# A hybrid decoder layer on one core: plain products in the first third of the tokens, weight sums formed over two thirds, quads accumulating in one bank

## The chip, the cores and the metric

The kernel runs on one core of one Trainium2 chip. The metric is device time in microseconds: the median of the timed runs. A core has a tensor engine (PE) that multiplies into PSUM (eight banks of 128 partitions x 512 fp32), a vector engine (DVE), a scalar engine (ACT), GpSimd (POOL), which does not take part in reading PSUM here, and SyncE (SP), whose queue issues every transfer of this kernel in the order of the program.

## The reference

One layer for 2048 prompt tokens and 8 x 8 sample tokens (2112 in all), width 1024, everything in fp32:

```python
xn = rms_norm(x, norm_pre)
z = einsum('btd,de->bte', xn, w_in)            # 1024 -> 4096
v_pool, g_pool, u_lru, g_lru = four blocks of 1024 columns of z
y_pool = causal multi-scale pooling of v_pool (windows 2, 4, 8, 16), a map per group, a scale
y_lru  = width-4 causal convolution of u_lru, then a gated linear recurrence (scan over tokens)
mixed  = concat(y_pool * silu(g_pool), y_lru * silu(g_lru))      # 2048
out    = einsum('bte,ed->btd', mixed, w_out)   # 2048 -> 1024
return x + rms_norm(out, norm_post), and the new states
```

## The kernel before

**Precision.** An fp32 operand is split into a high part (a copy to fp32r, usually on ACT) and a low part (a subtraction, on DVE or POOL); `split` (lines 127 to 132) does both. A product is high x high, high x low and low x high, three matmuls. `quad_product` (342) does this over four blocks of 128 rows: twelve matmuls of 128x128 by 128x352.

**Stages.** The tokens are cut in three thirds of 704 (m = 0, 1, 2). A start stage loads and normalizes the first third and makes the first pair of blocks of each of V, G and U by plain products (`z_pair`). Then come the quads of the three thirds in the order of `QUADS` (704 to 715), then an output stage (from 1582) that multiplies the stored `mixed` by `w_out`. This output stage works on sums of blocks of `w_out`, which `combos_chain` (1245) forms ahead and stores in `wtd`.

**A quad** is (m, p, kind): two blocks of 128 output columns (j = 0, 1) of one kind (V the pool input, G its gate, U the recurrent input, L its gate) over the 704 tokens (two halves of 352, c = 0, 1), with the inner 1024 in two halves (h = 0, 1). As a 2x2 matrix product it is made with seven products instead of eight (Winograd's form of Strassen's scheme), at the price of sums: of x (named T1 to T4, beside the plain quarters X11, X21, X22) and of the weights. `ORDER` gives the order of the products, `XOF` the x operand of each. `quad_slot` (863) issues one product and returns its evacuation: PSUM banks a, b, e, c, d, the intermediate sums in a tile `q` (`t["tmp"]`), five additions on DVE (516 ns each) and two copies on ACT. Product 2 accumulates onto bank a (used by product 1) and product 3 onto bank e (used by product 5); these carry line 236, the others 238.

**Weights.** For each quad of the first third, and the first three of the second, `w_step` (742) forms the four sums on DVE and splits the seven operands: the high parts on ACT, four low parts on POOL (`LO_POOL`) and three on DVE. Where m < 2 the split operands (512 KB each) are stored to `wsd`; all later quads load them from there. A weight step is taken seven products ahead of its use (`AHEAD`), in eight buffers (`W_BUFS`).

**Order of the work.** The program is written out by hand inside `manual_schedule`: each engine runs its queue in that order. `one_slot` (1284) is one product's time: it issues the product, then the evacuations of the slot before, one waiting map or gate from `pe_q`, due stores (`later`), and then as much of the side chains (`gens`, sorted by rank) as the planned budget of 1.92 us per engine allows (`run_gens`). The side chains are `pool_chain`, `silu_chain`, `conv_chain`, `lru_chain`, `x_chain` (normalizes the next third), `combos_chain` and `region_chain`. Weight steps and the `transition` (1202), which forms the next third's x operands during the last quad of a third and the first of the next, stand ahead of the slot's evacuations. Before a quad the program puts in empty slots until enough tiles are free (line 1499).

The main loop, in short:

```python
for n in range(7 * len(QUADS)):
    qi, i = divmod(n, 7)
    ...
    ws = w_step(n + AHEAD)
    one_slot(body, [a + b for a, b in zip(tr, ws)])
```

Of the kernel before, what the change touches and what calls it, by code (L numbers as in the profile page):

```python
# [18 lines left out]
KT = D // P  # L19
# [40 lines left out]
SLOTS = ("A", "B", "X11", "T2", "T1", "T3", "T4", "X21", "X22")  # L60
# [4 lines left out]
def hymba_kernel(  # L65
# [650 lines left out]
    LATE_PREP = [(1, 0, kind) for kind in "VGU"]  # L716
    PREP = [q for q in QUADS if q[0] == 0] + LATE_PREP
# [13 lines left out]
    def w_raw(q, names):  # L731
        if q is None:
            return
        _, p, kind = q
        for n in names:
            blk, h = blocks(kind, p)[int(n[0]) - 1], int(n[1]) - 1
            t = (raw_tile if n[0] == "1" else tp_tile)(f"wr{kind}{p}_{n}")
            w_rawt[q, n] = w_load_raw(blk, h, t)

    LO_POOL = (0, 3, 5, 6)  # L740

    def w_step(n):
        if n >= 7 * len(QUADS):
            return 0.0, 0.0, 0.0
        q, i = QUADS[n // 7], n % 7
        m, p, kind = q
        key = (KINDS[kind] // 8 * NG + p) * 7 + i
        t = w_tiles[n] = half_tile(f"w{m}{kind}{p}_{i}")
        flat = t.rearrange("p a b -> p (a b)").bitcast(F32)
        if q not in PREP:  # L750
            nc.sync.dma_start(out=flat, in_=wsd[:, key, :])
            return 0.0, 0.0, 0.0
        nxt = PREP[PREP.index(q) + 1] if q != PREP[-1] else None
        r = {n_: w_rawt.get((q, n_)) for n_ in ("11", "12", "21", "22", "s1", "s2", "s4")}
        cost = 0.65
        if i == 0:
            src = r["11"]
        elif i == 1:
            s1 = w_rawt[q, "s1"] = raw_tile(f"s1{kind}{p}")
            src = w_rawt[q, "s2"] = tp_tile(f"s2{kind}{p}")  # L760
            tadd(s1, r["21"], r["22"])
            tsub(src, s1, r["11"])
            cost += 1.3
        elif i == 2:
            src = r["s1"]
            tsub(r["21"], r["11"], r["21"])
            cost += 0.65
            w_raw(nxt, ("11",))
        elif i == 3:
            src = r["21"]  # L770
        elif i == 4:
            src = r["22"]
            s4 = w_rawt[q, "s4"] = raw_tile(f"s4{kind}{p}")
            tsub(s4, r["12"], r["s2"])
            cost += 0.65
        elif i == 5:
            src = r["12"]
        else:
            src = r["s4"]
        pool = i in LO_POOL  # L780
        split(t[:, 0, :], t[:, 1, :], src, AC, G if pool else V)
        if i == 3:
            w_raw(nxt, ("21",))
        elif i == 4:
            w_raw(nxt, ("22",))
        elif i == 5:
            w_raw(nxt, ("12",))
        if m < LM:
            later(2, lambda: nc.sync.dma_start(out=wsd[:, key, :], in_=flat))
        return cost - (0.65 if pool else 0.0), 0.62, (1.35 if pool else 0.0)  # L790
# [65 lines left out]
    def put_sum(q, j, c, a, b, op=ALU.add):  # L856
        for out, lo, hi, is8 in dst_parts(q, j, c):
            i0, i1 = a[:, lo:hi], b[:, lo:hi]
            if is8:
                i0, i1 = as8(i0), as8(i1)  # L860
            V.tensor_tensor(out=out, in0=i0, in1=i1, op=op)

    def quad_slot(q, i, n):
        t = Q[q]
        pid = ORDER[i]
        w = w_tiles.pop(n)
        name = XOF[pid]
        c0 = CW

        def bank(key):  # L870
            t[key] = z_psum(f"{key}{n}")[:, :CW]
            return t[key]

        def U(i):
            return t["tmp"][:, i * CW:(i + 1) * CW]

        if pid == 1:
# [10 lines left out]
        elif pid == 5:  # L888
            quad_product(bank("e"), w, name, True, True)

            def evac():
                pass
# [819 lines left out]
```

## Time and profile before

| | |
|---|---|
| runs | 1345.55, 1342.72, 1345.72 us; median 1345.55 |
| profiled execution | 1339.65 us, of which 1337.9 are the span from first to last instruction |
| busy, share of the span | PE 86%, weight load 80%, DVE 74%, ACT 48%, POOL 35% |
| transfers | 324.73 MB, 243 GB/s on average |
| granted clock of PE | 0.926 on average |

How to read the views: the list of lines groups instructions by line, engine and tile, with count, total time, mean nanoseconds of one, and the idle time of the engine just before them with who ended it. The list of waits has total, times and longest in microseconds. A row of the timeline has start, length, engine, line, and in brackets how long the engine stood idle before it. A weight tile is named by third and kind: `w0L` is a tile of kind L in the first third. Matmul ends in the timeline are modelled and overlap the next start; the distance of two starts is the time of one group.

### The profile page before, as it was taken

The numbers are of one execution on the slowest core, as the hardware profiler recorded it, in microseconds if no ns is written. First come the engines' busy times: TensorE is split into PE (matmuls) and PEld (weight loads), VectorE is DVE, ScalarE is ACT, GpSimd is POOL, SyncE is SP. The second block draws the span as 40 slices with busy tenths as digits, with TensorE's granted clock in tenths as the row PEclk, the third lists the DMA queues.
The fourth block names the chain that finished last, engine by engine and source line by source line (L and its number), as shares of the span: only waits on it lengthen the run. The fifth ranks groups of instructions, "written<-read, shape, count | busy, mean of one in ns | idle before, by whom it ended". The sixth has DMA issues, their size and how long they took to land. (4 is left out here: it accounts for less than half of the span.)

```text
span 1337.9 us, 17719 instructions
## 1 busy us (share of the span) xinstructions
PE 1152.4 (86%) x6118; PEld 1069.0 (80%) x6118; DVE 990.3 (74%) x1370; ACT 645.8 (48%) x1031; POOL 463.9 (35%) x408
## 2 busy tenths in 40 slices
PE   7949678857757699989899979899987999999996
PEld 6949678747757699989889869899975888887775
DVE  7899688888788568767676854857556758677668
ACT  5353757625643775444546452727654333334322
POOL 3366464554456323232244322424310002221222
PEclk9979779868878899989899979999988999999998
DMA  8067586945665799979789777978658966657653
GB/s 308 26 222 286 184 318 241 359 181 187 228 226 202 272 330 354 354 242 383 235 315 333 265 262 250 325 254 278 206 170 236 269 183 187 182 165 233 183 166 110
DMA packets 172010, 324.73 MB, mean 243 GB/s; under 512 B 17360, under 2 KB 79056, under 8 KB 171920
## 3 DMA queue, kind: packets, MB, share of 16 engines
q1 hardware_dynamic: 171920, 323.59, 70.8%
q8 instruction: 48, 0.79, 0.2%
q14 instruction: 42, 0.34, 0.1%
HBM read 221.13 MB, written 102.15 MB: 242 GB/s over the span
## 5 line engine op out<-in xcount | busy, mean ns | idle before, releaser
L442 PE MATMUL p<-XN,s 128*128 128x512 f32 (+1 forms) x224 | 88.3, 394 | 8.9 <-ACT s L129 8.7
L1059 DVE SCALAR_TENSOR_TENSOR xs<-u,parT,xs 128x704 f32<-128x704 f32 (+1 forms) x72 | 88.3, 1227 | 3.8 <-ACT xs L1049 2.6
L444 PE MATMUL p<-XN,s 128*128 128x512 f32 (+1 forms) x224 | 88.0, 393 | 2.0 <-DVE s L132 2.0
L443 PE MATMUL p<-XN,s 128*128 128x512 f32 (+1 forms) x224 | 88.2, 394 | 0.4 <-DVE XN L132 0.2
L1100 POOL TENSOR_TENSOR ig<-ig,xs 128x704 f32<-128x704 f32 (+1 forms) x24 | 46.2, 1927 | 94.7 <-ACT ig L1099 80.6
L435 POOL TENSOR_TENSOR xr<-acw,xr 128x512 f32<-128x512 f32 x8 | 13.1, 1641 | 185.9 <-DVE acw L575 123.5
L238 PE MATMUL y<-dh,pw 128*128 128x352 f32 x192 | 56.5, 339 | 15.5 <-ACT pw L129 14.9
L307 POOL TENSOR_TENSOR xl<-xs,xh 128x704 fp32r<-128x704 f32 (+1 forms) x24 | 45.6, 1902 | 66.6 <-ACT xh L1064 53.4
L435 POOL TENSOR_TENSOR xr<-ac,xr 128x512 f32<-128x512 f32 x19 | 35.6, 1887 | 79.8 <-issue 52.2
L435 DVE TENSOR_TENSOR a<-a,a 128x512 f32<-128x512 f32 x48 | 34.0, 714 | 37.0 <-DMA a<-mixed 32.4
L129 ACT CAST s<-a 128x512 fp32r<-128x512 f32 x48 | 28.6, 618 | 67.1 <-DVE a L435 48.9
L1064 ACT CAST xh<-xs 128x704 fp32r<-128x704 f32 (+1 forms) x24 | 18.9, 788 | 86.1 <-DVE xs L1059 86.1
L238 PE MATMUL z<-XN,w 128*128 128x352 f32 x288 | 53.3, 347 | 7.4 <-ACT w L1316 5.4
L442 PEld LDWEIGHTS p<-XN,s 128*128 128x128 f32 x224 | 43.0, 192 | 19.3 <-ACT s L129 9.1
L238 PEld LDWEIGHTS z<-XN,w 128*128 128x128 f32 x288 | 49.9, 203 | 10.3 <-ACT w L1316 5.4
L1108 DVE SCALAR_TENSOR_TENSOR w<-rg,xs 128x704 f32<-128x704 f32 (+1 forms) x24 | 22.9, 955 | 43.5 <-ACT xs L1105 36.8
L444 PE MATMUL p<-XN,a 128*128 128x512 f32 x137 | 54.3, 396 | 0.1
L442 PE MATMUL p<-XN,a 128*128 128x512 f32 x137 | 54.2, 396 | 0.0
L443 PE MATMUL p<-XN,a 128*128 128x512 f32 x137 | 54.2, 395 | 0.0
L444 PEld LDWEIGHTS p<-XN,s 128*128 128x128 f32 x224 | 42.9, 191 | 12.2 <-DVE s L132 2.7
L310 DVE TENSOR_TENSOR q<-b,q 128x352 f32<-128x352 f32 x45 | 23.2, 517 | 38.8 <-PE b L238 37.2
L443 PEld LDWEIGHTS p<-XN,s 128*128 128x128 f32 x224 | 43.0, 192 | 10.7 <-DVE XN L132 1.1
(481 smaller groups left out, 3704.0 us busy)
## 6 DMA issues: line engine op xcount, KB each, us to landing
a<-mixed SPq DMA_DIRECT2D x112, 256.0 KB, 4.2
mixed<-g SPq DMA_DIRECT2D x48, 352.0 KB, 5.0
wsd<-w0L SPq DMA_DIRECT2D x28, 512.0 KB, 4.9
w1L<-wsd SPq DMA_DIRECT2D x28, 512.0 KB, 6.0
w2V<-wsd SPq DMA_DIRECT2D x28, 512.0 KB, 5.7
w2G<-wsd SPq DMA_DIRECT2D x28, 512.0 KB, 5.8
w2U<-wsd SPq DMA_DIRECT2D x28, 512.0 KB, 4.9
w2L<-wsd SPq DMA_DIRECT2D x28, 512.0 KB, 7.1
```

Source lines behind the costliest of these rows:

```text
L129: hi_eng.copy(out=hi, in_=src)
L238: nc.tensor.matmul(out, lhsT=lhsT, rhs=rhs, start=start, stop=stop)
L307: (eng or V).tensor_tensor(out=out, in0=a, in1=b, op=ALU.subtract)
L310: (eng or V).tensor_tensor(out=out, in0=a, in1=b, op=ALU.add)
L435: (eng or nc.vector).tensor_tensor(out=out, in0=a, in1=b, op=op)
L442: nc.tensor.matmul(out, lhsT=ah, rhs=wh, start=start and k == 0, stop=False)
L443: nc.tensor.matmul(out, lhsT=ah, rhs=wl, start=False, stop=False)
L444: nc.tensor.matmul(out, lhsT=al, rhs=wh, start=False, stop=stop and k == KT - 1)
L1059: V.scalar_tensor_tensor(out=xs, in0=E[:, k:k + n], scalar=col(C_CW + 8 * k, b), in1=xs, op0=ALU.mult, op1=ALU.add)
L1064: AC.copy(out=xh, in_=xs)
L1100: G.tensor_tensor(out=gi, in0=gi, in1=v, op=ALU.mult)
L1108: V.scalar_tensor_tensor(out=u, in0=r, scalar=1.0, in1=v, op0=ALU.add, op1=ALU.mult)
```

## The change

- In the first third a quad is made of its eight plain products. Two products (h = 0, 1) accumulate in one bank, and four copies on ACT take the banks out. No sums of x and no sums of weights are needed for it: each quad splits four weight tiles, one quad ahead (`plain_tile`, in slots 4 to 7), three of which are stored for later thirds.
- The weight sums for the later thirds are formed in the first third for the six V and G quads (`s_prep`, in slots 0 to 3, into x regions that lie idle) and in the second third for its ten other quads (`is_late`), which load their three plain operands from `wsd` and form and store four others.
- All low parts of weights are formed on DVE; none on POOL.
- In the later thirds, products 1, 6, 7 and 4 accumulate in one bank a, and 5 and 3 in e; after each, the running result is copied by ACT or added into its place by DVE. A quad has four copies on ACT and three additions on DVE, and needs no tile `q`.
- The x operands of a third are formed in another order, and those of the start stage are the four plain quarters; the start stage stores its split weights too.
- The sums of `w_out` (`combos_chain`) move from the second third to the last, load one step ahead and wait less; `region_chain` starts earlier there.

The diff, cut to its core:

```diff
-AHEAD = 7
-ORDER = (1, 6, 5, 7, 4, 2, 3)
+ORDER = (1, 5, 6, 3, 7, 2, 4)
...
+    EARLY = "VG"
+    def is_late(q):
+        return q[0] == 1 and (q[1] == 0 or q[2] not in EARLY)
...
+    PLAIN_PID = {"11": 1, "12": 2, "22": 4}
+    IDLE = [XN[:, BASE[n] + 1024 * i:BASE[n] + 1024 * (i + 1)] for n in ("X11", "T2", "T1") for i in range(2)]
...
+    def plain_tile(q, n):
+        t = w_tiles[q, n] = half_tile(f"w{q[2]}{q[1]}_{n}")
+        split(t[:, 0, :], t[:, 1, :], w_rawt[q, n], AC, V)
+        if n in PLAIN_PID:
+            store_w(flat_of(t), q[2], q[1], PLAIN_PID[n])
+        return 0.65, 0.62, 0.0
...
+    def s_sums(q, i):
+        r11, r12, r21, r22 = (w_rawt[q, n] for n in NAMES)
+        if i == 0:
+            tadd(r22, r21, r22)
+        elif i == 1:
+            tsub(r21, r11, r21)
+        elif i == 2:
+            tsub(r11, r22, r11)
+        else:
+            tsub(r12, r12, r11)
...
+    def s_prep(q, i):
+        if q[2] not in EARLY:
             return 0.0, 0.0, 0.0
+        s_sums(q, i)
+        dve, act = 0.65, 0.0
+        for pid in ((), (5,), (6, 7), (3,))[i]:
+            b = IDLE[n_idle[0] % len(IDLE)]
+            n_idle[0] += 1
+            split(b[:, :512], b[:, 512:], w_rawt[q, S_OF[pid]], AC, V)
+            store_w(b, q[2], q[1], pid)
+            dve, act = dve + 0.65, act + 0.62
+        return dve, act, 0.0
+
+    def w_step(q, i):
         m, p, kind = q
+        pid = ORDER[i]
+        t = w_tiles[q, pid] = half_tile(f"w{m}{kind}{p}_{pid}")
+        if not is_late(q) or pid in (1, 2, 4):
+            key = (KINDS[kind] // 8 * NG + p) * 7 + pid - 1
+            nc.sync.dma_start(out=flat_of(t).bitcast(F32), in_=wsd[:, key, :])
+        if not is_late(q) or i > 4:
             return 0.0, 0.0, 0.0
+        if i < 4:
+            s_sums(q, i)
+        if not i:
+            return 0.65, 0.0, 0.0
+        split(t[:, 0, :], t[:, 1, :], w_rawt[q, S_OF[pid]], AC, V)
+        store_w(flat_of(t), kind, p, pid)
+        return 1.3 if i < 4 else 0.65, 0.62, 0.0
...
+    PLAIN = [(j, h, c) for c in range(2) for j in range(2) for h in range(2)]
+    PLAIN_X = {(0, 0): "X22", (1, 0): "T3", (0, 1): "X21", (1, 1): "T4"}
+    def plain_slot(q, i):
...
+        if h == 0:
+            t["z"] = z_psum(f"z{q[2]}{q[1]}_{i}")[:, :CW]
+        quad_product(t["z"], w, PLAIN_X[h, c], h == 0, h == 1)
...
+            if h:
+                put_copy(q, j, c, z)
...
+        key = {1: "a", 6: "a", 7: "a", 4: "a", 5: "e", 3: "e", 2: "d"}[pid]
+        first = pid in (1, 5, 2)
+        if first:
+            t[key] = z_psum(f"{key}{q[0]}{q[2]}{q[1]}")[:, :CW]
+        z = t[key]
+        quad_product(z, w, XOF[pid], first, True, True)
+
+        def evac():
+            if pid == 1:
+                put_copy(q, 0, 0, z)
+            elif pid == 5:
+                put_copy(q, 1, 1, z)
+            elif pid == 6:
+                put_copy(q, 0, 1, z)
+            elif pid == 3:
+                put_sum(q, 0, 1, z)
+            elif pid == 7:
+                put_sum(q, 1, 1, z)
+            elif pid == 2:
+                put_sum(q, 0, 0, z)
+            else:
+                put_copy(q, 1, 0, z)
+                quad_end(q)
...
+        plan = {0: (("X11",), ("T1",), ("t1", "T2"), ("t2",), ("X22-", "T3"), ("t3",), ("T4",), ("X21-",), ("4", "t4")),
...
     def combos_chain():
-        for k in range(KT):
+        def load(k):
...
+        nxt = load(0)
+        yield 0, 0, 0, 3
+        for k in range(KT):
+            r, nxt = nxt, load(k + 1) if k + 1 < KT else None
...
+                yield 0.65, 0, 0, 0
+            yield 0, 0, 0, 3
...
+        def start_store(kind, b):
+            for n, pid in PLAIN_PID.items():
+                store_w(flat_of(wt[b + int(n[0]) - 1, int(n[1]) - 1]), kind, 0, pid, 0)
+            due_dmas()
...
+        def prep(n, qi, i):
+            if QUADS[qi][0] == 0:
+                if i < 4:
+                    return s_prep(QUADS[qi], i)
+                if qi < lasts[0]:
+                    return plain_tile(QUADS[qi + 1], NAMES[i - 4])
+                if i == 4:
+                    for s in steps[:3]:
+                        w_step(*s)
+                return w_step(*steps[i - 1])
+            n = n - i0 + 7
+            return w_step(*steps[n]) if n < len(steps) else (0.0, 0.0, 0.0)
...
-                while t_free() < {"V": 1}.get(q[2], 3) or (q[2] == "V" and (e_free() < 2 or not sums_done(*q[:2]))):
+                while t_free() < {"V": 0}.get(q[2], 2) or (q[2] == "V" and (e_free() < 2 or not sums_done(*q[:2]))):
...
+                if qi + 1 < len(QUADS) and QUADS[qi + 1][0] == 0:
+                    w_raw(QUADS[qi + 1])
+                if qi + 2 < len(QUADS) and is_late(QUADS[qi + 2]):
+                    w_raw(QUADS[qi + 2])
...
-            if m == 1 and (qi, i) == (lasts[0] + 5, 0):
-                spawn(combos_chain(), 0, rank=3)
             if m == 2 and (qi, i) == (lasts[1] + 2, 0):
+                spawn(region_chain(0, "b11", 0, 5), 0, rank=2)
+                spawn(combos_chain(), 20, rank=2)
```

More of the change, by code (lines that the diff above doesn't have):

```diff
@@ new lines, in store_w, with flat_of @@
+    def store_w(flat, kind, p, pid, slots=2):
+        key = (KINDS[kind] // 8 * NG + p) * 7 + pid - 1
+        later(slots, lambda: nc.sync.dma_start(out=wsd[:, key, :], in_=flat.bitcast(F32)))
+    def flat_of(t):
+        return t.rearrange("p a b -> p (a b)")
+    def plain_tile(q, n):
[4 more added lines that the diff above has]
+        return 0.65, 0.62, 0.0
@@ L1263, in region_chain @@
+                later(2, lambda j=j, k=k, o=r[o]: nc.sync.dma_start(out=wtd[:, j, k, :], in_=o))
+                yield 0.65, 0, 0, 0
+            yield 0, 0, 0, 3
     def region_chain(r, j, k0, k1):
@@ L1444, in hymba_kernel @@
         scaled("G", ZG0, 0)
+        start_store("V", 0)
         for b in (16, 17):
```

256 lines of the change are left out of this document (79 added, 177 removed).

## Prediction

> **What bounds the kernel now.** I read the page's busy shares and slices first, then split the span into stages where the matmul timeline shows the first product of each third.
>
> ```profile
> PE 1152.4 (86%) x6118; PEld 1069.0 (80%) x6118; DVE 990.3 (74%) x1370; ACT 645.8 (48%) x1031; POOL 463.9 (35%) x408
> PE   7949678857757699989899979899987999999996
> PEclk9979779868878899989899979999988999999998
> ```
>
> ```profile
> 0.00:63.51 63.51, 55.11 (x302) 51.96 (x303) 48.26 (x98) 28.08 (x63) 24.24 (x40) 1.00 0.49 171
> 63.51:391.05 327.54, 232.22 (x1253) 225.15 (x1251) 276.14 (x307) 178.46 (x274) 174.96 (x122) 0.84 0.67 244
> 391.05:691.74 300.69, 267.51 (x1576) 264.40 (x1576) 218.25 (x259) 155.58 (x222) 99.50 (x88) 0.94 0.83 299
> 691.74:969.20 277.46, 258.18 (x1549) 255.53 (x1548) 187.49 (x252) 146.42 (x199) 102.46 (x122) 0.96 0.78 268
> 969.20:1337.90 368.70, 339.39 (x1444) 271.98 (x1444) 260.18 (x458) 137.22 (x275) 62.72 (x39) 0.96 0.64 189
> ```
>
> The columns are length; PE, weight load, DVE, ACT, POOL busy; clock; DMA share; GB/s. The page's PE share of 86% is an average over unlike stages: the first third's 13 quads take longer (327.54) than the second's 16 (300.69) or the last's 16 (277.46), at the lowest clock, with DVE at 276.14/327.54 = 0.84 and POOL at its highest. What a quad must cost PE shows in undisturbed products:
>
> ```profile
> 105.37 2.08 PE L238 MATMUL b<-XN,w0V 128*128 128x352 f32 x12
> 107.29 2.08 PE L238 MATMUL e<-XN,w0V 128*128 128x352 f32 x12
> ...
> 487.79 0.32 PE L238 MATMUL r<-xh,lw 128*128 128x352 f32 x1
> 488.75 2.08 PE L238 MATMUL b<-XN,w1G 128*128 128x352 f32 x12
> ```
>
> Starts are 1.92 us apart, so seven products are 13.44; a map or gate between two products (487.79 to 488.75) is 0.96. A third has 16 map and 16 gate groups; from the loops, the first third's window holds about 24 of its 32, the rest falls into the next. PE's own work is thus 13 x 13.44 + 24 x 0.96 = 197.8 in the first third and 16 x 13.44 + 32 x 0.96 = 245.8 in the others. Lost: 129.8, 54.9 and 31.7 us. Who was waited for in the first third, by the list of waits (total, times, longest):
>
> ```profile
> PE e L236 <- DVE g L861: 42.4, 7, 11.6
> PE e L236 <- DVE e L861: 10.1, 3, 4.9
> PE a L236 <- ACT q L882: 8.9, 2, 7.6
> ```
>
> and in the second and the last:
>
> ```profile
> PE e L236 <- DVE g L861: 19.2, 5, 7.9
> ...
> PE e L236 <- DVE g L861: 9.5, 2, 5.5
> ```
>
> The seventh product accumulates in bank e, which must first be read by DVE; DVE is late. Each long wait is paid twice:
>
> ```profile
> 98.77 3.89 PE L236 MATMUL e<-XN,w0L 128*128 128x352 f32 x12 [4.45 <-DVE g L861]
> ...
> 119.36 2.19 PE L236 MATMUL e<-XN,w0V 128*128 128x352 f32 x12 [1.32 <-DVE e L861]
> ```
>
> After 4.45 us idle a product takes 3.89 instead of 2.08; after 1.32 it takes 2.19. The Trainium skill (TensorE: Matmul & The Clock Gate, "What's actually happening") says the clock halves after an idle window of about 3.4 us and returns after as long a busy one; the trace agrees. Why DVE is late:
>
> ```profile
> L310 DVE TENSOR_TENSOR s1G<-wrG,wrG 128x512 f32<-128x512 f32 x3 | 5.6, 1868 | 0.0
> L310 DVE TENSOR_TENSOR s1L<-wrL,wrL 128x512 f32<-128x512 f32 x3 | 2.0, 678 | 0.0
> ...
> L310 DVE TENSOR_TENSOR q<-b,q 128x352 f32<-128x352 f32 x13 | 6.7, 515 | 0.0
> ```
>
> On ACT and on POOL in the same third:
>
> ```profile
> L129 ACT CAST w0L<-wrL 128x512 fp32r<-128x512 f32 x15 | 8.8, 610 | 1.2 <-DVE wrL L307 1.2
> L882 ACT COPY q<-a 128x352 f32<-128x352 f32 x13 | 5.8, 445 | 0.0
> ```
>
> ```profile
> L132 POOL TENSOR_TENSOR w0L<-wrL,w0L 128x512 fp32r<-128x512 f32 x11 | 22.6, 2057 | 39.6 <-ACT w0L L129 39.3 <-POOL u L838 0.3
> L132 POOL TENSOR_TENSOR w0G<-wrG,w0G 128x512 fp32r<-128x512 f32 x9 | 13.4, 1496 | 4.4 <-ACT w0G L129 3.1 <-DMA swd<-lw 1.3
> ```
>
> The same sum takes 678 ns in one place and 1868 in another, and this third is where POOL is busy for 174.96 us. The Trainium skill (SBUF — State Buffer, "Who interferes with whom") calls it an exclusive port: a DVE instruction with two inputs in SBUF and a POOL instruction reading SBUF exclude each other. The two rows fit that.
>
> **First third, part by part.** PE: eight products instead of seven, 13 x 1.92 = +25.0; own work 222.7. The 13 x 5 additions on PSUM leave DVE (65 x 0.515 = -33.5); four copies per quad take their place on ACT, two more than now (26 x 0.445 = +11.6 there, beside PE work). Weights on DVE: 98 instructions now (13 x 7, and 7 of the next third's first quad), after it 13 x 4 low parts, 6 x 8 for sums and splits of the V and G quads, 8 ahead: 108. Their price lies between 0.678 and 1.868; now they come to some 96 us (29 rows, of which s1G and s1L above are the dearest and one of the cheapest), 0.98 each. I take 0.85, since some 54 POOL splits between 1.5 and 2.06 us, some 94 of its 175 us, go: 92 us. At 0.68 it would be 73, at 0.98 106. The first quad no longer needs sums of x (about a dozen instructions of 0.8 to 1.6 us, -10). DVE's other 136 us should lose a tenth to the quieter port (bounds nothing and a fifth): -14. DVE: 276.1 - 33.5 - 4 - 10 - 14 = 215. By the rule of the Trainium skill's SBUF page alone, the instructions freed from POOL would all run at their lone price: an estimate of some 180 us, with PE the only bound.
>
> The wait that carried the loss is gone: two products share a bank, no product accumulates on a bank that has been read, and a weight tile is split four slots (7.7 us) before it is used, which replaces "seven ahead". At today's 0.84 DVE share 215 us make 255 us; PE's 222.7 plus the 31.7 that the last third loses make 254. I take 255, -72.5; ends 231 (8 us lost) and 289 (242.6 us of DVE, nothing gained in its prices, at 0.84). The 39 us that the first quad takes now (63.51 to 102.45) fall to near 16 in this: its x parts are plain halves, the last two are needed only from the fifth product on.
>
> **SP's queue and the stores.** Nine 512 KB stores of the start's weights go into SP's queue ahead of the raw loads of the first quad; a wait there for a split holds those loads back. PE has the two last products of the start to run meanwhile (48 matmuls of 0.16 us each, 15.4 us together), so I cost it at nothing; without that cover a few us. In the third itself stores fall from 91 to 63.
>
> **Second third.** Ten quads instead of three form sums here. Without the 8 instructions done ahead (7 now) these are 72 on DVE instead of 14: at 0.85 each 61 us against some 15. Off DVE: 16 x 2 additions (-16.5), and the output weights' sums, 20 of which lie here:
>
> ```profile
> L307 DVE TENSOR_TENSOR wo<-wo,wo 128x512 f32<-128x512 f32 x20 | 22.3, 1115 | 0.1
> ```
>
> and by the list of DMA issues:
>
> ```profile
> wo<-in_w_out SPq DMA_DIRECT2D x32, 256.0 KB, 6.0
> wtd<-wo SPq DMA_DIRECT2D x32, 256.0 KB, 5.8
> ```
>
> DVE: 218.3 + 46 - 16.5 - 22.3 = 225. ACT: 16 x 2 copies (+14) and 22 splits (+13): 183. The new wait is the shared bank: products 1, 6, 7, 4 run in bank a, each after the evacuation of the one before, with one product (1.92 us) between; 3 follows 5 likewise. Today product 2 comes four products after product 1 in bank a, and product 3 has two products between it and the one (7) whose evacuation reads bank e. Behind a waiting product stands all of PE's queue, maps and gates too, and the sums on DVE wait for those. The evacuations are queued on ACT and DVE behind weight splits, where ACT itself waits for DVE's sums. How late they come today:
>
> ```profile
> 426.48 2.10 PE L238 MATMUL a<-XN,w1G 128*128 128x352 f32 x12
> 436.69 0.45 ACT L882 COPY q<-a 128x352 f32<-128x352 f32 x1
> ...
> 535.60 2.09 PE L238 MATMUL a<-XN,w1V 128*128 128x352 f32 x12
> 537.73 0.45 ACT L882 COPY q<-a 128x352 f32<-128x352 f32 x1 [5.34 <-PE a L238]
> ```
>
> The product that ends at 428.58 is copied by 437.14, 8.6 us later; the other by 0.5. I took this lag for product 1 (ACT) and 7 (DVE) in all 32 quads of both later thirds; these two pairs are among the longest and shortest. What exceeds 1.92 us, the larger of both per quad, sums to 44.5 and 33.2; by the present two-product allowance it is 30.7 and 23.7. So the tighter chain costs about +14 and +10. Against that, the second third starts without the backlog of the first, and its x sums are formed in the order of use while plain products still run: I take -15. DVE's extra 7 us fall beside PE work. 300 us; ends 277 (the last third's loss) and 322 (nothing won at its start, chain and DVE's 7 on the path).
>
> **Last third.** +10 for the chain, -16.5 on DVE for additions, +20 sums of the output weights at 0.68 to 1.12 (14 to 22 us): DVE level. All 64 transfers of 256 KB now fall here, at up to twice their pace (a set of four sums needs about five slots instead of nine). The 40 of them that lie earlier today are 10.5 MB; with the present 268 GB/s x 277.46 us = 74.4 MB that makes 298 GB/s over 285 us, less than:
>
> ```profile
> 468.56:567.40 98.84, 98.38 (x616) 97.90 (x615) 74.42 (x99) 54.93 (x83) 28.95 (x29) 1.00 0.95 346
> ```
>
> where PE did not wait. But in their stretch of some 80 us, 2.1 MB per five slots on top of 268 is beyond 346. Weights are asked for seven products (13.4 us) ahead, so I charge little: 288; ends 270 (chain at nothing, additions saved) and 310 (the chain's 10 and 22 of sums on the path). Start and output stage keep 63.5 and 368.7.
>
> **Sum.** 63.5 + 255 + 300 + 288 + 368.7 = 1275 span, +1.75 around it: 1277, against the profiled 1339.65. The median shown, 1345.55, lies 0.4% above that execution; I stay near the profiled frame and say 1276.
>
> **Rivals.** *PE-bound throughout*: if DVE runs free of POOL as the 678 ns row has it, the first third takes 240, the second 277, the last 270: 63.5 + 240 + 277 + 270 + 368.7 + 1.75 = 1221. For: DVE's room; against: 0.84 without slack. 12%. *DVE stays the pace of the first third*: with prices unchanged 289, total 1311. For: six quads have twelve DVE instructions each. 10%. *Transfers of the output weights collide with weight loads in the last third*: 310 there, 1299. 8%.
>
> *The shared bank locks PE to ACT and DVE* (the slower end): the ten quads with sums then run at the first third's present pace, 327.54/13 = 25.2 us, instead of 300.69/16 = 18.8: +64; the 22 others each lose a half-clock product, 3.89 - 1.92 = 1.97: +43. 1384. It decides from an extra wait of 63/32 = 2.0 us per quad. Against it, product 1 is copied within 0.54 us in eight of the second third's sixteen quads. 5%.
>
> *Short waits lower the clock*: four small waits a quad, each below what the rows show to hurt, could still add up to one slow product in each of 32 quads, +63: 1340, no change. The Trainium skill's clock page ("A second HAM failure mode: psum-queue depth-cycling") has such an oscillation from micro-idles between groups. The 2.19 us row speaks against it. 3%.
>
> **Numbers.** The forecast case, within 1245 to 1305, has 62%. Faster by over 0.3% (about what a measurement here can tell): 62 + 12 + 10 + 8 = 92%; same 3%; slower 5%. The range, 1238 to 1318, takes in the collision and the DVE case and leaves out most of the PE-bound one and the last two.
>
> **What would show it.** Right: the first third near 255 with no idle of PE before products of DVE's making, DVE's 128x512 instructions near 0.7 to 0.9 us, POOL near 80 us there, the clock above 0.9. New waits of PE on ACT's and DVE's evacuations of bank a in the ten quads of the second third, mostly of 1 to 3 us, which stays near 300. Wrong: the first third over 290, the later two together over 620, or waits for weight loads in the last.

## The result and the profile after

The changed kernel takes 1295.49 us (median of 1295.17, 1295.49 and 1297.61), against 1345.55: a ratio of 0.9639, 95% interval 0.9614 to 0.9664. It is faster, 20 us slower than the 1276 forecast, and inside the range. The profiled execution is that of 1295.17 us, with a span of 1293.5.

The page, in the rows shown of before (busy times, the span in 40 slices, the granted clock):

```profile
PE 1167.0 (90%) x6274; PEld 1080.5 (84%) x6274; DVE 901.0 (70%) x1300; ACT 683.5 (53%) x1138; POOL 327.6 (25%) x340
PE   7999989998689897988889997899889999999987
PEclk9999989999799997998999998999998999999989
```

The same five stages as before, cut where the first product of each third starts (length; PE, weight load, DVE, ACT, POOL; clock; DMA share; GB/s):

```profile
0.00:63.69 63.69, 54.45 (x302) 51.13 (x303) 48.53 (x101) 32.65 (x67) 20.96 (x40) 1.00 0.67 247
63.69:313.03 249.34, 238.35 (x1432) 234.16 (x1431) 194.08 (x237) 165.20 (x267) 72.35 (x66) 0.97 0.71 257
313.03:632.98 319.95, 268.90 (x1527) 260.63 (x1527) 218.50 (x267) 186.36 (x283) 83.21 (x77) 0.92 0.75 269
632.98:930.00 297.02, 267.72 (x1580) 263.39 (x1578) 182.79 (x245) 163.43 (x250) 90.34 (x120) 0.95 0.83 291
930.00:1293.50 363.50, 337.58 (x1438) 271.17 (x1438) 257.15 (x453) 135.91 (x273) 60.69 (x39) 0.96 0.65 192
```

Stage by stage the change is +0.2, -78.2, +19.3, +19.6 and -5.2, in all -44.4 of span. (The output stage, whose code is nearly untouched, read 363.5 to 369.4 in the runs of the changed kernel that leave it alone: its -5 is nothing to explain. The windows don't hold quite the same work: the second third has 49 matmuls fewer than before, 0.16 us each, and the last 31 more, as maps and gates of one third run on into the next.) So the first third gave 78 us and the other two gave half of it back. Who held PE there, by the lists of waits of the second and of the last third, and what held DVE in the last:

```profile
PE a1V L235 <- ACT e L878: 12.5, 2, 12.1
PE a1L L235 <- ACT g L878: 8.5, 5, 2.7
PE a1G L235 <- DVE g L874: 7.9, 3, 3.8
PE e1L L235 <- ACT g L878: 5.9, 4, 2.7
...
PE a2U L235 <- ACT u L878: 9.3, 3, 5.3
PE a2V L235 <- DVE e L874: 8.0, 1, 8.0
```

```profile
DVE wo L306 <- DMA wo<-in_w_out: 25.3, 6, 8.8
```

The waits have the shape that the prediction named: a product of the shared banks a or e, released by the copy (L878) or addition (L874) that empties the bank. The ten rows of the second third come to 51 us (one of them, 3.1 us, is a wait for a weight split); the longest single one is 12.1 us at its start. The DVE row is new: before, DVE waited 2.5 us in all for the loads of the output weights.

### The profile page after: what moved, and what is told of

It reads as the page before. It is cut to its first block, busy times and chain, and to the rows that moved or that the text cites. A ratio compares the mean times of both kernels' runs of the same rounds, so it can differ in the third digit from the quotient of the medians.

```text
span 1293.5 us, 17899 instructions
## 1 busy us (share of the span) xinstructions
PE 1167.0 (90%) x6274; PEld 1080.5 (84%) x6274; DVE 901.0 (70%) x1300; ACT 683.5 (53%) x1138; POOL 327.6 (25%) x340
## 5 line engine op out<-in xcount | busy, mean ns | idle before, releaser
L1072 DVE SCALAR_TENSOR_TENSOR xs<-u,parT,xs 128x704 f32<-128x704 f32 (+1 forms) x72 | 84.7, 1183 | 15.7 <-ACT xs L1062 12.7
L237 PE MATMUL zL<-XN,wL 128*128 128x352 f32 x384 | 64.9, 328 | 2.1 <-ACT wL L128 1.9
L237 PEld LDWEIGHTS zL<-XN,wL 128*128 128x128 f32 x384 | 63.2, 192 | 2.7 <-ACT wL L128 2.2
L441 PEld LDWEIGHTS p<-XN,s 128*128 128x128 f32 x224 | 43.3, 193 | 18.8 <-ACT s L128 9.1
L306 POOL TENSOR_TENSOR dl<-s,dh 128x704 fp32r<-128x704 f32 x24 | 39.3, 1638 | 63.0 <-ACT dh L1004 42.7
L237 PE MATMUL zU<-XN,wU 128*128 128x352 f32 x288 | 50.6, 331 | 4.5 <-ACT wU L128 2.3
L443 PEld LDWEIGHTS p<-XN,s 128*128 128x128 f32 x224 | 43.1, 192 | 13.1 <-DVE s L131 3.3
```

Source lines behind the costliest of these rows:

```text
L237: nc.tensor.matmul(out, lhsT=lhsT, rhs=rhs, start=start, stop=stop)
L306: (eng or V).tensor_tensor(out=out, in0=a, in1=b, op=ALU.subtract)
L441: nc.tensor.matmul(out, lhsT=ah, rhs=wh, start=start and k == 0, stop=False)
L443: nc.tensor.matmul(out, lhsT=al, rhs=wh, start=False, stop=stop and k == KT - 1)
L1072: V.scalar_tensor_tensor(out=xs, in0=E[:, k:k + n], scalar=col(C_CW + 8 * k, b), in1=xs, op0=ALU.mult, op1=ALU.add)
```

## What the waits stand for: the theories

Waits that end with an evacuation of a shared bank do not say what made the evacuation late. **Lock theory**: it is the bank, because one product of slack is too little. **Load theory**: ScalarE and VectorE are late with everything, because ten quads' sums and splits (and, in the last third, the output weights' sums) run through the same in-order queues; the bank only shows it. **Collision theory**, for the last third: the chain of the output weights is the whole loss. A fourth, **T2**, for the 12 us at the second third's start, came out of the trace.

Times of all runs, with the three thirds (first product to first product) of the profiled execution. Ratios are against the kernel before on the same chip.

| run | us | ratio (95%) | first | second | last |
|---|---|---|---|---|---|
| before | 1345.55 | 1 | 327.5 | 300.7 | 277.5 |
| after | 1295.49 | 0.9639 (0.9614-0.9664) | 249.3 | 320.0 | 297.0 |
| own banks | 1288.15 | 0.9593 (0.9566-0.9621) | 247.1 | 316.9 | 288.5 |
| evacuations first | 1288.97 | 0.9585 (0.9561-0.9609) | 250.0 | 312.3 | 294.3 |
| no late sums | 1258.87 | 0.9357 (0.9339-0.9375) | 246.9 | 287.0 | 290.8 |
| no late sums, own banks | 1254.86 | 0.9328 (0.9311-0.9344) | 249.3 | 287.2 | 285.7 |
| five quads' sums early | 1317.38 | 0.9799 (0.9774-0.9824) | 286.2 | 308.1 | 292.0 |
| transition on DVE | 1291.34 | 0.9604 (0.9570-0.9638) | 248.8 | 318.9 | 295.1 |
| longer pause | 1287.79 | 0.9573 (0.9545-0.9601) | 246.9 | 321.6 | 285.6 |
| no output-weight sums | 1278.08 | 0.9502 (0.9481-0.9523) | 247.2 | 323.1 | 277.1 |
| before, low parts on DVE | 1355.14 | 1.0075 (1.0053-1.0096) | 323.7 | 314.0 | 279.6 |
| plain low parts on POOL | 1310.90 | 0.9750 (0.9698-0.9802) | 266.3 | 318.0 | 294.7 |
| three edits | 1280.36 | 0.9518 (0.9475-0.9561) | 250.6 | 310.7 | 286.9 |
| four edits | 1281.28 | 0.9521 (0.9505-0.9537) | 253.7 | 306.7 | 290.1 |

How much of a third's time is chance shows where a run leaves that third's code as in after: the second read 318.0 to 323.1 (four profiles), the last 290.8 to 297.0 (four).

## The second third: bank, order or load

**Own banks.** Products 6, 7 and 4 get a bank each. Two pairs still share: 2 follows 1 in bank a, five products later, and 3 follows 5 in bank e, two products later, as in the changed kernel.

```diff
-        key = {1: "a", 6: "a", 7: "a", 4: "a", 5: "e", 3: "e", 2: "d"}[pid]
-        first = pid in (1, 5, 2)
+        key = {1: "a", 2: "a", 5: "e", 3: "e", 6: "b", 7: "c", 4: "d"}[pid]
+        first = pid not in (2, 3)
...
+            elif pid == 7:
+                d10 = dst_parts(q, 1, 0)[0][0]
...
+                put_sum(q, 1, 1, d10)
+                put_sum(q, 0, 1, t["e"])
```

> The changed kernel, with the bank sharing alone undone in the second and last third: each of the five products that begin a sum has a bank of its own, the sums of products are formed by VectorE in the output tiles (two 352-column additions a quad more on VectorE, two copies fewer on ScalarE). Plain first third, late sums and the later loads of the output weights stay. Theory (the shared bank locks TensorE to the evacuations in ScalarE's and VectorE's queues): the waits of TensorE on banks a and e in the second third fall from about 44 us to under 15, the second third from 320 to 295-302 us, the last from 297 to 285-290; in all about 1260-1275 us. Rival 1 (the ten late quads' sums and splits are the load, whoever has the bank): the waits only move to weight tiles or to other banks, the second third stays over 312; in all 1288-1300, or longer through the 20 us that VectorE gains a third. Rival 2 (loads of the output weights that hold VectorE up): the last third stays at 297.

By stage, the second and the last third, and PE's waits of the second:

```profile
310.50:627.40 316.90, 265.50 (x1528) 261.88 (x1527) 233.71 (x292) 181.75 (x268) 86.35 (x76) 0.90 0.76 270
627.40:915.94 288.54, 262.80 (x1573) 259.80 (x1571) 209.93 (x301) 156.08 (x224) 98.40 (x121) 0.96 0.85 301
```

```profile
PE e1V L235 <- ACT e L878: 19.1, 2, 12.0
PE e1L L235 <- ACT g L878: 18.1, 4, 6.6
PE e1U L235 <- ACT u L878: 9.0, 3, 4.3
```

No product waits on bank a any more, and the total is the same 51 us: the waits moved to product 3, the only one that still comes soon (two products) after a copy out of its bank. The lateness shows wherever a short slack is left. In the second third, 1 us below the unchanged ones, that is rival 1; in the last, 288.5 is what the lock theory gave, 2 us below the lowest unchanged one. But in this run VectorE's wait for the output weights' loads fell as well, from 25.3 to 9.3 us, so the gain of the last third need not be the bank's.

**Evacuations first.** The function `ahead` is called inside the slot, behind the evacuations.

```diff
-            tr = transition(m if qi in lasts[:2] else m - 1, ti) if ti >= 0 else used
-            ws = prep(n, qi, i)
-            one_slot(lambda: quad_slot(q, i), [a + b for a, b in zip(tr, ws)])
+            def ahead():
+                tr = transition(m if qi in lasts[:2] else m - 1, ti) if ti >= 0 else [0.0, 0.0, 0.0]
+                ws = prep(n, qi, i)
+                return [a + b for a, b in zip(tr, ws)]
+            one_slot(lambda: quad_slot(q, i), ahead)
```

> The changed kernel, with one order turned in each slot of the later two thirds: the evacuations of the slot before are issued ahead of that slot's weight sums, splits and transition steps, so that on ScalarE and VectorE no split stands ahead of a copy out of the shared bank. Theory (it is the order in the queues that makes the lock cost): waits on banks a and e in the second third from about 44 to under 25 us, the second third 320 to about 300-305, in all 1270-1280 us. Rival 1 (the load of the sums and splits, not the order): the waits stay, some of them now on weight tiles; within 5 us of 1295. Rival 2 (the time from a product's end to its copy's end is itself too long for a slack of one product): within 5 us of 1295 with the waits on the same banks at the same operations.

The second third took 312.3: the fall is half of what the theory gave, and the total of 1288.97 lies between the theory's range and the rivals'. Its waits, in the four largest rows:

```profile
PE a1G L235 <- DVE g L874: 13.6, 4, 4.9
PE a1V L235 <- ACT e L878: 9.8, 1, 9.8
PE a1L L235 <- ACT g L878: 6.4, 3, 2.7
PE e1U L235 <- ACT u L878: 4.9, 3, 2.5
```

Over all rows, waits ended by ScalarE's copies fell from 38.6 to 25.0 us, and those ended by VectorE's additions rose from 9.4 to 17.9. The order in the queues matters, for 6 to 11 us by the unchanged ones; beyond that, one engine's lateness takes the place of the other's.

**No late sums** (leaves out the ten quads' sums and their splits, and with them 40 raw loads and 40 stores) and **no late sums, own banks**.

```diff
-        if not is_late(q) or pid in (1, 2, 4):
-            key = (KINDS[kind] // 8 * NG + p) * 7 + pid - 1
-            nc.sync.dma_start(out=flat_of(t).bitcast(F32), in_=wsd[:, key, :])
-        if not is_late(q) or i > 4:
-            return 0.0, 0.0, 0.0
+        src = 1 if is_late((1, p, kind)) and pid in S_OF else pid
+        key = (KINDS[kind] // 8 * NG + p) * 7 + src - 1
+        nc.sync.dma_start(out=flat_of(t).bitcast(F32), in_=wsd[:, key, :])
+        return 0.0, 0.0, 0.0
...
-                if qi + 2 < len(QUADS) and is_late(QUADS[qi + 2]):
-                    w_raw(QUADS[qi + 2])
```

> The changed kernel with work left out: the ten late quads' 40 weight sums are neither formed nor split; their four sum tiles are loaded from the stored first tile of the same quad instead (the output is then not the reference's). From the second third go some 40 sums and 40 low parts of VectorE (about 55 us), 40 high parts of ScalarE (25 us), 40 raw loads and 40 stores; the banks, the evacuations and the transitions stay. Load theory (ScalarE and VectorE, each in order and waiting for one another, are late with everything while they carry the late sums, and the bank only shows it): TensorE's waits fall from 51 to under 25 us, the second third from 320 to 285-295, in all 1262-1272. Lock theory (the shared bank's slack of one product is the price): waits on banks a and e stay over 35 us, the second third over 308; in all over 1283. The last third, which reads stored tiles already, stays at 297 under both.

> Both at once: the ten late quads' sums left out as in the run beside it (the output is not the reference's), and products on banks of their own. Under the load theory the banks add nothing once the load is gone: the second third within 4 us of the run with the load alone left out. If the lock has a price of its own under light load, it comes out here: the second third 8 us or more below that run, and the last third 285-290 as with own banks alone.

The second third of the two, in this order:

```profile
310.00:597.00 287.00, 262.03 (x1552) 256.74 (x1551) 166.65 (x191) 163.28 (x240) 82.20 (x79) 0.96 0.81 268
```

```profile
313.00:600.20 287.20, 259.31 (x1552) 257.08 (x1551) 179.25 (x215) 153.66 (x222) 81.79 (x76) 0.95 0.79 266
```

This tells the theories apart. With the shared bank untouched, taking away 51.9 us of DVE and 23.1 us of ACT takes 33 us off the third (31 to 36 by the unchanged ones), and PE's listed waits there come to 25 us instead of 51 (the total, 1258.87, is 3 us below the load theory's range). The transfers that go as well are hardly the cause: in that third of the changed kernel PE, VectorE and ScalarE together wait 1.3 us for transfers. With the load gone, own banks change the second third by 0.2 us. So the late sums' load costs the second third some 33 us, and sharing bank a has next to no price of its own there. For bank e this isn't shown: products 5 and 3 share it in every run, and with own banks and no late sums all of PE's 27.9 us of listed waits are on it. In the last third own banks read 5 us less here (285.7 for 290.8; VectorE's wait for the output weights is again shorter, 9.7 us for 23.6) and 2 to 8 less above, at the edge of what chance does.

**Five quads' sums early.**

```diff
-        return q[0] == 1 and (q[1] == 0 or q[2] not in EARLY)
+        return q[0] == 1 and (q[1] == 0 or q[1:] == (NG - 1, "L"))
...
-        if q[2] not in EARLY:
+        if is_late((1,) + q[1:]):
```

> The changed kernel, with five of the ten late quads' weight sums (20 sums, 20 splits) formed in the first third instead of the second; banks, order in the slot and loads stay. They are 20 x 0.69 + 20 x 0.9 = 32 us of VectorE and some 13 us of ScalarE that move. Rival 1 (load of the late sums): the second third falls by 20-30 us, the first, where VectorE has 55 us idle, grows by 3-10; in all 1270-1280 us. Theory (the shared bank's lock): a part of the waits goes with the splits that stand ahead of the copies, 5-12 us of the 51, and the first third grows as much; in all 1285-1297.

Neither. The second third fell by 11.9, and the first grew by 36.9. Of that, 28 us come before its last plain product has been issued (277.2 us after the third's start, in after 249.2), mostly in its second half: PE's listed waits for split weight tiles are 18 us there, for 8 in after. Some 9 come at its end, where ScalarE waits for a load, VectorE behind it for a transition step, and PE for a stored tile:

```profile
341.80 0.62 ACT L128 CAST pw<-pwr 128x512 fp32r<-128x512 f32 x1 [11.51 <-DMA pwr<-in_pool_w]
343.72 1.62 DVE L306 TENSOR_TENSOR XN<-XA,XN 128x1408 fp32r<-128x1408 f32 x1 [12.71 <-ACT XN L321]
351.70 3.51 PE L235 MATMUL a1V<-XN,w1V 128*128 128x352 f32 x12 [8.69 <-DMA w1V<-wsd]
```

So the sums are not free in the first third either, where VectorE and ScalarE also split the plain tiles. The run does not show whether fewer of them would be, nor why the loads at the end came late.

## The stall at the second third's start

The timeline of after, from the third's first product; a1V is bank a of the first quad:

```profile
313.14 3.82 POOL L306 TENSOR_TENSOR XN<-XA,XN 128x1408 fp32r<-128x1408 f32 x1
313.85 3.66 DVE L309 TENSOR_TENSOR wr1V<-wr1V,wr1V 128x512 f32<-128x512 f32 x1
...
325.95 3.86 POOL L306 TENSOR_TENSOR XN<-XA,XN 128x1408 fp32r<-128x1408 f32 x1 [8.99 <-ACT XN L321]
326.72 3.85 DVE L306 TENSOR_TENSOR rt<-XA,rt 128x704 f32<-128x704 f32 x1
...
333.56 0.45 ACT L878 COPY e<-a1V 128x352 f32<-128x352 f32 x1
334.06 3.89 PE L235 MATMUL a1V<-XN,w1V 128*128 128x352 f32 x12 [12.12 <-ACT e L878]
```

Bank a is full at 315; its copy runs at 333.56, behind eighteen microseconds of transition steps and weight splits in ScalarE's queue, which themselves wait for VectorE. Twice VectorE takes over 3.6 us for a short instruction, just while GpSimd runs one of 3.8. **Transition on DVE** takes these two GpSimd instructions away:

```diff
-            x_lo(name, src, eng)
+            x_lo(name, src, V)
```

> The changed kernel, with the low parts of two token quarters (X22, X21) in each transition on VectorE, in their old place of the order, not on GpSimd: two 128x1408 operations of 3.8 us a transition leave GpSimd, 2 x 1.63 = 3.3 us come to VectorE. Theory T2, formed from the trace (the first copy out of bank a of the second third stands on ScalarE behind a high part that waits for VectorE, and VectorE's 0.69 us sum took 3.66 us and its 1.8 us difference 3.85 us, each just while GpSimd ran such an operation): these two shrink to under 1 and 2 us, TensorE's wait of 12.1 us at 334 goes below 6, the second third 320 to 308-314 us, the last by 2-5 as its transition has the same; in all 1277-1287. Rival (the transition's work itself is too much for VectorE and ScalarE, whichever engine helps): the wait stays at 10-15 us and the third gains nothing or grows by 3; in all 1293-1302.

```profile
315.13 0.68 DVE L309 TENSOR_TENSOR wr1V<-wr1V,wr1V 128x512 f32<-128x512 f32 x1
...
325.02 0.88 DVE L306 TENSOR_TENSOR rt<-XA,rt 128x704 f32<-128x704 f32 x1
...
330.24 0.45 ACT L878 COPY e<-a1V 128x352 f32<-128x352 f32 x1
...
330.74 3.78 PE L235 MATMUL a1V<-XN,w1V 128*128 128x352 f32 x12 [10.20 <-ACT e L878]
```

Half of T2 holds: 3.66 became 0.68 and 3.85 became 0.88. The other half falls: the wait went from 12.1 to 10.2 us, the second third reads 318.9, and the ratio's interval overlaps that of after. VectorE works through the transition with gaps under 1 us in both; the work that stands ahead of the copy is most of the stall, not the stretching of two instructions in it. With the evacuations first as well (three edits, below) the longest wait there is 6.5 us.

## The last third: the output weights' chain

**Longer pause**, and **no output-weight sums** (leaves out the chain's loads, differences and stores; the output reads plain parts of `w_out`).

```diff
-            yield 0, 0, 0, 3
+            yield 0, 0, 0, 7
```

```diff
-                spawn(combos_chain(), 20, rank=2)
...
-            src = wtd[:, j, k, :]
+            src = w_out[k * P:(k + 1) * P, PIECE * (j % 2):PIECE * (j % 2 + 1)]
```

> The changed kernel, with one number changed: the chain that forms the output weights' combinations in the last third pauses seven slots instead of three between a block's load and its use. Rival 2 (VectorE, in order, is held by the loads' arrival and with it the copies out of the banks): VectorE's 25 us of waiting for these loads goes below 8, the last third falls by 8-15 us, in all 1280-1288 us. Theory (VectorE's wait is taken out of its idle time, TensorE is held by the shared bank): the wait goes, the last third stays within 3 us; in all 1292-1298.

> The changed kernel with work left out: the chain that forms the output weights' combinations (32 loads, 32 differences of 0.87 us on VectorE, 32 stores in the last third) isn't run, and the output reads plain parts of the weights in their place (the output is not the reference's). Collision theory (what the last third lost against before is the chain that was put into it): the last third falls from 297 to 275-281 us, the 277 of before; in all 1274-1281. Lock theory (the shared bank took it): 284-292, as much as the longer pause alone gave (285.6); in all 1282-1290.

With the pause, DVE's wait for these loads and the last third; then the last third without the chain:

```profile
DVE wo L306 <- DMA wo<-in_w_out: 1.3, 1, 1.3
```

```profile
633.20:918.84 285.64, 264.26 (x1580) 260.97 (x1578) 179.90 (x245) 162.25 (x249) 87.00 (x120) 0.96 0.85 303
```

```profile
634.20:911.25 277.05, 260.50 (x1579) 256.81 (x1578) 154.95 (x213) 161.87 (x249) 90.56 (x120) 0.98 0.77 252
```

The pause came out as its rival 2 had it, and the run without the chain as the collision theory had it. Without the chain the last third takes 277.05, before's 277.46: the chain is the whole loss, 14 to 20 us. Of these, 5 to 11 come from differences that reach the head of VectorE's queue before their operands, with the additions that empty PE's banks queued behind them (`a2V <- DVE e` fell from 8.0 to 0.5 us); one number in a `yield` removes that part, and the ratio's interval (to 0.9601) lies below that of after (from 0.9614). The rest, 285.6 for 277.05, may be the chain's 25 us on VectorE or its 64 transfers; this was not taken apart. Own banks on top of the pause do not add: 290.1 in the run of four edits, for 286.9 in that of three.

## What made the first third

**Before, low parts on DVE** does one part of the change alone, **plain low parts on POOL** undoes it alone.

```diff
-    LO_POOL = (0, 3, 5, 6)
+    LO_POOL = ()
```

```diff
-        split(t[:, 0, :], t[:, 1, :], w_rawt[q, n], AC, V)
+        split(t[:, 0, :], t[:, 1, :], w_rawt[q, n], AC, G)
```

> The kernel before, with one part of the change alone: the low parts of all weight splits on VectorE (seven products, their banks and their sums stay as before). In the first third 38 low parts leave GpSimd, where they took 1.50 to 2.06 us each (64.5 us), and add 38 x 0.69 to 1.02 = 26-39 us to VectorE's 276. Theory (what the first third gained is VectorE's time, and GpSimd's operations stretch VectorE's own, so that taking them away pays for most of what it adds): VectorE ends at 280-305 us of the first third, the third stays within 12 us of its 327.5; in all 1330-1350 us. Rival (products' own banks were the gain; the split's place matters little): within 3 us of 1344. Rival (VectorE bound by its count of instructions): the first third goes to 345-365 us, in all 1360-1380.

> The changed kernel, with one part alone undone: the low parts of the plain weight tiles (48 in the first third, 0.87 to 1.02 us each on VectorE, 44 us) go back to GpSimd, at the 1.50 to 2.06 us that they took there before: GpSimd's 72 us become 145-170. Theory (GpSimd beside VectorE stretches VectorE's operations, and its low parts arrive too late for the products): the first third 249 to 262-280 us, with waits of TensorE on the plain weight tiles; in all 1307-1330. Rival (the plain products' slack and their banks made the gain, wherever the splits run): the first third within 4 us of 249; in all 1291-1299.

First and second third of the one, first of the other:

```profile
63.70:387.40 323.70, 236.62 (x1251) 228.30 (x1250) 267.61 (x361) 181.87 (x278) 85.69 (x70) 0.84 0.68 250
387.40:701.40 314.00, 270.63 (x1577) 267.04 (x1575) 218.79 (x273) 156.30 (x221) 80.31 (x77) 0.91 0.80 286
```

```profile
63.80:330.10 266.30, 243.75 (x1432) 237.85 (x1431) 183.60 (x191) 165.88 (x268) 147.26 (x119) 0.96 0.67 243
```

In the old scheme VectorE does 54 instructions more (361 for 307; the expectation's 38 were those split from raw tiles alone) in 8.5 us less (267.6 for 276.1): GpSimd's 89 us had cost VectorE more than the work it took over. But the third gains only 3.8 us, since the seven-product chain is still there (PE's listed waits at L236, on banks a and e, come to 62 us), and the kernel is 0.75% slower for 13.3 us in the second third, which no theory had. There PE waits twice for a gate's x operand, 6.7 and 8.7 us (`r <- ACT xh`, `r <- POOL xl`), waits that before doesn't have; why they come late isn't shown. In the new scheme the move back of the plain tiles' 48 low parts costs 17.0 us, as the theory had it, with PE waiting on tiles that GpSimd makes late (`zU <- POOL wU` 6.8 us, `zL <- POOL wL` 4.2). So of the 78 us, some 17 hang on these low parts being on VectorE, and some 61 are there with them on GpSimd. How these 61 divide between banks, missing sums of x, missing weight sums and the sums' low parts (which stay on VectorE here) was not taken apart.

## The edits together

**Three edits**: evacuations first, longer pause, transition on DVE. **Four edits**: own banks as well.

> The changed kernel with three of the edits together: evacuations ahead of the slot's splits, seven slots between load and use of the output weights, the transitions' low parts on VectorE. If the three act on different waits, their gains add: -6.5 and -7.7 (as measured alone) and what the third gives alone (theory T2: -8 to -18), so 1263-1273 us. If they act on the same wait, or the transition's gives nothing: 1278-1285.

> The changed kernel with four edits together: the three of the run before (1280.4 us) and banks of their own for the products, with two more additions a quad on VectorE. If the bank still holds TensorE once the order, the pause and the transition are mended: 1268-1276. If own banks only move the waits to another bank, as in the second third of the run with own banks alone: 1278-1286, since VectorE has 20 us a third more.

Three together take 1280.36 us, ratio 0.9518 (0.9475 to 0.9561): the interval lies below that of after, and the version beats both kernels by some 1% and 5%. The -6.5 and -7.7 of two edits add (1281.3 by sum), the transition's gives nothing on top. Own banks add nothing either: the second third reads 4 less, the last 3 more, VectorE being busy 6 us more in the one and 28 more in the other.

## Why the prediction held, and which term was off

The stages miss by -6, +20, +9 and -5 us (the last is the output stage's scatter), so that the total is nearer than its parts.

- **First third: right, and one of its two sums by luck.** 255 forecast, 249.3 measured. PE's long waits for DVE's additions are gone (its listed waits come to 11 us, none over 2.2), the clock is 0.97, POOL 72 us (near 80 said), DVE 194 (215 said). The 128x512 instructions of DVE took 0.86 each on average, 0.85 said, but there are 96 of them and not 108; and the others lost more than a tenth (the 18 of `xs<-u,parT,xs` went from 1381 to 1081 ns). Two sums met at 255. DVE's, at a share of 0.84, would have given 231 with the measured 194: DVE was not the pace. PE's sum is the one that holds, with other terms: 184 matmuls of maps and gates instead of 144, and 20 us lost instead of 31.7. The first quad, 39 us before and near 16 by the forecast, is eight products in one unbroken row:

```profile
63.69 15.52 PE L237 MATMUL zL<-XN,wL 128*128 128x352 f32 x96
```

- **Second third: the size was off, by 20.** The busy times were close (DVE 225 said, 218.5 measured; ACT 183 and 186.4). What failed is the sentence that DVE's added work falls "beside PE work", and the -15 for a start without backlog. Run without the late sums, the third takes 287: 75 us of work on two engines that are busy 68% and 58% of the time cost PE 33 us. Each runs in order, and the waits show each held by the other: VectorE's low parts wait for ScalarE's high parts (the two rows below, after's second third), ScalarE's high parts wait for VectorE's sums (5.1 us for `wr1V`, 5.0 for `wr1L`), and the copies out of the banks queue behind. The start, instead of giving 15, holds the 12.1 us stall.

```profile
DVE w1L L131 <- ACT w1L L128: 22.5, 15, 4.3
DVE w1U L131 <- ACT w1U L128: 13.3, 9, 3.6
```

- **The chain: smaller than costed.** +14 and +10 were charged to the tighter banks. Banks of their own for products 6, 7 and 4 are worth 1 to 6 us in the second third, nothing there once the load is gone, and 2 to 8 in the last, nothing there once the pause is longer. What the shared bank e costs isn't shown.
- **Last third: 288 said, 297.0 measured.** The output weights' chain was called level on DVE and charged little for its transfers; it costs 14 to 20 us. The rival of the colliding transfers had the right chain, but the wrong victim: no weight load is waited for by PE in the last third; VectorE waits, and PE behind it. That its total, 1299, lies near is chance: it had the last third at 310 and the second at 300.
- **Rivals.** The lock of PE to ACT and DVE, 1384, would have eaten the gain from 2.0 us more per quad on; the second third lost 19.3/16 = 1.2, and to load. PE-bound throughout (1221) would need both later thirds free of waits, as they are not. DVE as pace of the first third (1311) fell with DVE at 194. Short waits did lower the clock, but half as often as that rival had it: 10 and 6 stretches of halved clock in the two later thirds, not one in each of 32 quads.

## What to carry to other kernels

A wait that ends with an evacuation names the last link, not the load: test it by taking out the load that shares the evacuating engine's queue before giving the waiter more banks. Two in-order engines that hand pieces to each other held a third here while busy 68% and 58%, so moved work costs something even on an engine that looks idle; cost it by what stands behind it in the queue. And in such a queue the distance between a load and its first use is worth checking first: one number gave some 8 us of the whole here.

## What the runs showed of the hardware

**VectorE waits out a GpSimd instruction.** The sum that started at 313.85 ended 0.55 us after GpSimd's instruction did (313.14 + 3.82 = 316.96; 317.51), and the difference of 326.72 ended 0.76 us after (329.81; 330.57): about their own 0.68 and 0.88 us, run behind the other. The Trainium skill (SBUF — State Buffer, "Who interferes with whom") calls the shared port an exclusive lock; the trace agrees.

**The clock is halved in steps of 3.41 us, by how busy PE was in the step before.** Two products of the changed kernel with nearly the same wait before them:

```profile
818.35 2.18 PE L235 MATMUL e2L<-XN,w2L 128*128 128x352 f32 x12 [1.72 <-ACT g L878]
```

```profile
447.04 3.31 PE L235 MATMUL e1U<-XN,w1U 128*128 128x352 f32 x12 [1.79 <-ACT u L878]
```

Over all fourteen timelines, of the groups of twelve matmuls with an idle of 1 to 5 us before them, longer than 2.6 us were 3 of 50 after 1.0 to 1.5 us of idle, 20 of 49 after 1.5 to 2.0, 24 of 32 after 2.0 to 2.5, 61 of 75 after 2.5 to 3.5, and 39 of 39 beyond. There is no sharp bound for a wait at the 3.4 us that the prediction took from the Trainium skill's page TensorE: Matmul & The Clock Gate, "What's actually happening"; the page speaks of an idle window of that length, and calls it free-running.

The granted clock in the traces shows such steps, and that a step need not be idle. Each of the 280 stretches of halved clock that end within the fourteen traces lasts one to six times 3.41 us, and all changes of one trace lie on one grid of that length. From 60 us on, of the full-clock steps in which PE was busy less than 45% of the time 255 of 256 are followed by a halved one, of those at 45 to 55% 23 of 68, and of the 3992 above that none. A halved step is followed by another after each of 182 steps under 80% busy, after 13 of 24 at 80 to 85%, and after none of 267 above. So a wait of under 3.41 us halves the clock if enough of it falls into one step. Here are the step that holds the wait of 1.79 us and the next one, then the step that holds the wait of 1.72 us and the next; the columns are those of the stages above, with PE busy first and the clock third from the end:

```profile
444.33:447.74 3.41, 1.62 (x10) 1.33 (x9) 1.71 (x2) 3.39 (x5) 0.67 (x1) 1.00 1.02 418
447.74:451.15 3.41, 3.41 (x14) 3.41 (x13) 2.00 (x4) 2.76 (x5) 1.50 (x2) 0.50 0.63 253
816.38:819.79 3.41, 1.69 (x11) 1.44 (x10) 2.68 (x3) 3.37 (x6) 2.88 (x5) 1.00 1.06 394
819.79:823.20 3.41, 1.13 (x7) 0.84 (x6) 0.74 (x1) 3.36 (x5) 0.00 (x0) 1.00 1.03 399
```

Both waits leave PE busy for nearly half of their step, where either can follow.
